# A hybrid decoder layer on one core: constant products in TensorE's pauses between the output projection and the first expert tile, and a refitted order

## The chip, the cores and the metric

The kernel runs on one core of one Trainium2 chip. The time is device time of one execution in microseconds, the median of several runs. The engines are TensorE (PE in the profile, its weight loads PEld), VectorE (DVE), ScalarE (ACT), GpSimd (POOL) and SyncE (SP, which here only issues DMAs). Each engine works through its own queue in order and waits for the others by semaphores.

## The reference

One layer over 512 tokens of width 1024, in float32. After a norm and one input projection, a state-space group (S5) and a sparse attention group work side by side. Their normed outputs meet in one output projection. A mixture of 32 experts follows, two per token.

```python
h = rms_norm(x, norm1_g[l])
proj = h @ w_in[l]
y_ssm = s5_mixer(proj[..., :D_SSM], ...)
y_att = nsa_mixer(proj[..., D_SSM:], ...)
mix = jnp.concatenate([rms_norm(y_ssm, out_g_ssm[l]), rms_norm(y_att, out_g_att[l])], axis=-1)
x = x + mix @ w_out[l]
x = x + hier_moe(rms_norm(x, norm2_g[l]), w_grp[l], b_grp[l], w_exp[l], b_exp[l],
                 w_gate[l], w_up[l], w_down[l])
```

In `hier_moe` a token's group is the one with the largest of 4 logits, and inside it the two best of 8 experts; each expert is `silu(t @ w_gate) * (t @ w_up)` times `w_down`.

## The kernel before

The tokens lie in four blocks of 128. Each part of the layer is a Python generator that yields one instruction (or a `Seq` of several) at a time: `proj`, `s5a`, `s5b`, `gelu`, `glu` (the gated unit behind S5), `scores`, `values`, `outproj`, `top2`, `route`, `expert` and others. `Sched.run` holds all live generators. At each step it works out for each one when its next instruction could start, by its own costs of instructions and the buffers' readiness, adds the generator's number from the table `PRIO`, and issues the one with the smallest sum. So the order on every engine is fixed when the program is built. In before.py `run` is at line 274, the table at 48.

`glu` multiplies by the gate's weights in PSUM tile `g` (`g<-yTh,gh` and so on), lets POOL add up the squares in `sq`, and multiplies them by a column of ones (`g<-ones,sq`). Behind it `wo` loads the weights of the output projection; `outproj` (line 1421) computes it in two parts, S5's first, attention's second, block by block into tiles `g` and `a`. `resid` adds the results to x on DVE.

`top2`, four times, transposes the new x of a block (`t<-ident`), multiplies it with the routing weights (128x36), and finds group and experts on DVE in many small steps. `norm2` makes the normed block on ACT, POOL and DVE and stores it to DRAM (`h2d`). `route` sums up positions with products of `A` and the constants `onesb` and `tri`, and from these the token list `gi` of 16 tiles: tile j serves experts j and j + 16, 64 tokens each. Its helper `weights` makes the table `tabw` with another eight products. `expert` (line 1705) gathers the tokens of a tile (`sc<-h2d,gi`), transposes them in two halves (`turn`), multiplies them with gate and up weights (16 products of 64 rows and 512 columns), then silu, transposes, and the down product. More tokens for an expert go to an overflow tile; `spill` computes its indices on DVE and, with `g<-R,oh`, on PE.

The expert weights are 96 tiles of 1 MB. `prefetch` issues their loads on SP in the order of use as soon as a buffer is free (pools `sa`, `sb`, `sc`, 26 of 1 MB, which the earlier parts share). An expert gives back two of them after each half of its gate products.

Of the kernel before, what the change touches and what calls it, by code (L numbers as in the profile page):

```python
# [27 lines left out]
for _n, _w in (("g1", 8), ("lre", 48), ("lim", 48), ("lst", 48), ("dsk", 8), ("bglu", 4), ("gq", 1),  # L28
# [9 lines left out]
NW = 10  # L38
NPS = 3, 2, 1, 2
NP = 4  # L40
DS = 1
SPILL_AT = 4
SC = 2, 4, 6, 8, 10, 12
# [1 line left out]

PRIO = {"proj": -3.72, "wsplit": 0.29, "xsplit": -0.08, "norm1": 0.04, "sink_u": 0.55, "sink_q": -0.76,
        "sink_gt": 3.61, "sink_k": -0.06, "s5": 0.19, "s5a": -0.69, "bcload": -9.42, "toeplitz": -18.02,
        "s5in": -0.17, "gelu": -0.12, "s5b": -0.75, "glu": -1.41, "compress": -0.96, "scores": -0.93,  # L50
        "scale": 0.37, "values": -0.25, "cmp": 0, "finish": -0.24, "wo": -1.28, "outproj": 0.02, "resid": -0.73,
        "norm2": -29.18, "top2": -0.61, "weights": 1.96, "place": -109.89, "prep": 1.2, "route": -1.71,
        "consts": -11.11, "scatter": -0.86, "base": -5.49, "moe": 43.94, "master": -5.48, "start": -35.5,
        "wload": -4.37, "prefetch": 3.58, "static": 2.45, "spill": -2.7}

# [54 lines left out]
class Sched:  # L112
# [12 lines left out]
    def spawn(self, gen, bias=0.0):  # L125
        self.th.append([gen, PRIO.get(gen.__name__, 0.0) + bias, None, None])

# [146 lines left out]
    def run(self):  # L274
        while self.th:
            moved = True
            while moved:
                moved = False
                for h in list(self.th):
                    while h[2] is None or callable(h[2]):  # L280
                        if h[2] is not None and not h[2]():
                            break
                        moved = True
                        try:
                            h[2] = next(h[0])
                        except StopIteration:
                            self.th.remove(h)
                            break
                        if isinstance(h[2], Seq):
                            h[3] = Seq()  # L290
                            h[3].extend(self.info(x[0]) for x in h[2])
                        else:
                            h[3] = None if callable(h[2]) else [self.info(x) for x in h[2]]
            best = None
            for h in self.th:
                if callable(h[2]):
                    continue
                _, s, f = self.pick(h)
                if best is None or s + h[1] < best[0]:
                    best = (s + h[1], s, f, h)  # L300
            if best is None:
                if self.th:
                    raise RuntimeError("stuck: " + ", ".join(
                        f"{h[0].__name__}:{h[0].gi_frame.f_lineno}" for h in self.th) )
                return
            self.cur = best[3][0]
            self.issue(best[1], best[2])
            best[3][2] = None
# [15 lines left out]
class Layer:  # L324
# [905 lines left out]
    def scores(self):  # L1230
# [38 lines left out]

        D = DS  # L1270
        for n in range(len(items) + D):
# [149 lines left out]
    def outproj(self):  # L1421
        V, S, G, T, Q = self.eng
        yield self.until("ys")
        for part in range(2):
            if part:
                yield self.until("ya")
            yh, yl, rs = (self.yah, self.yal, self.rsb) if part else (self.ysh, self.ysl, self.rsa)
            order = [(b, nh) for b in (3, 2, 1, 0) for nh in range(2)] if part else \
                [(b, nh) for nh in range(2) for b in (3, 2, 1, 0)]
            for b, nh in order:  # L1430
                if part:
                    yield self.until(f"ya{b}")
                i = 2 * part + nh
                yield lambda: i in self.wos
                hi, lo = self.wos[i]
                p = yield from self.ps(("g", "a") if part else "g", [128, 512])
                bs = slice(128 * b, 128 * b + 128)
                for k in range(0, 4, 2):
                    yield Seq(*(self.mm3(p, yh[:, i, bs], yl[:, i, bs], hi[:, i], lo[:, i], i == 0, i == 3)
                                for i in (k, k + 1)))  # L1440
                self.spawn(self.resid(p, rs, b, nh, part))
                if b == 0:
                    self.done(hi, lo)
                    if not part:
                        self.need["wo"] += 2
            self.done(yh, yl)
            if not part:
                self.flags.add("part0")

    def resid(self, p, rs, b, nh, part):  # L1450
        V, S, G, T, Q = self.eng
        if part:
            yield self.until(f"x{b}{nh}", f"r{b}")
        xv = self.xb[b][:, 512 * nh:512 * nh + 512]
        yield V.scalar_tensor_tensor(xv, p, rs[:, b:b + 1], xv, op0=OP.mult, op1=OP.add)
        self.done(p)
        self.flags.add(f"{'y' if part else 'x'}{b}{nh}")
# [247 lines left out]
    def expert(self, gi, oi, wv, ws, flag=None, tok=None):  # L1705

        V, S, G, T, Q = self.eng
        gx = yield from self.gather(gi)
        self.flags.add(flag)
        gT = yield from self.alloc("gT", [128, 8, 128])  # L1710
        yield from self.turn(gx, gT, 0)
        yield from self.turn(gx, gT, 1)
        self.done(gx)
        ph = yield from self.ps("a", [128, 512])
        for i in range(2):
            w = yield from ws(i)
            n = 128 // len(w)
            sls = [slice(n * s, n * s + n) for s in range(len(w))]
            yield Seq(*(T.matmul(ph[sl], gT[:, 4 * i + k, sl], wt[:, 512 * k:512 * k + 512],
                                 start=i + k == 0, stop=i == 1 and k == 3)  # L1720
                        for k in range(4) for sl, wt in zip(sls, w)))
            self.done(*w)
        self.done(gT)
        a = yield from self.alloc("h", [128, 256])
        yield S.activation(a, ph[:, 0:256], AF.Silu)
        yield V.tensor_mul(a, ph[:, 256:512], a)
        self.done(ph)
        aT = yield from self.alloc("hT", [128, 2, 128])
        pa = yield from self.ps("g", [128, 2, 128])
        yield Seq(*(T.transpose(pa[:, f], a[:, 128 * f:128 * f + 128], self.ident) for f in range(2)))  # L1730
        yield self.cp(aT, pa)
        self.done(pa, a)
        if tok is None:
            y = yield from self.alloc("z", [128, 1024])
        else:
            yh = yield from self.alloc("y", [128, 1024])
            yl = yield from self.alloc("y", [128, 1024])
        w = yield from ws(2)
        yield self.until("tabw")
        for nh in range(2):  # L1740
            py = yield from self.ps("a", [128, 512])
            yield Seq(*(T.matmul(py[sl], aT[:, f, sl], wt[:, 1024 * f + 512 * nh:1024 * f + 512 * nh + 512],
                                 start=f == 0, stop=f == 1) for f in range(2) for sl, wt in zip(sls, w)))
            c = slice(512 * nh, 512 * nh + 512)
            if tok is None:
                yield self.cp(y[:, c], py, wv)
            else:
                h = yh[:, c].bitcast(FR)
                yield S.activation(h, py, AF.Copy, scale=wv)
                yield V.scalar_tensor_tensor(yl[:, c].bitcast(FR), py, wv, h, op0=OP.mult, op1=OP.subtract)  # L1750
            self.done(py)
        self.done(aT, *w)
        if tok is None:
            yield self.until("base")
            yield G.indirect_dma_start(out=self.out, out_offset=bass.IndirectOffsetOnAxis(ap=oi, axis=0),
                                       in_=y, in_offset=None, compute_op=OP.add)
            self.done(y)
        else:
            self.spawn(self.scatter(tok, yh, yl))
# [222 lines left out]
def layer(ctx: ExitStack, tc: tile.TileContext, x, xt, win, pk, bcd, wglu, wck1, wck2, wcv1, wcv2,  # L1982
# [24 lines left out]
    L.hnq = [L.tmp.tile([128, 48], F32, name=f"hnq{i}") for i in range(2)]  # L2007
    L.need = {"P": NP, "ya": 2, "xs": 2, "comp": 2, "yT": 1, "ysl": 2, "wo": 5, "moe": 5, "spill": 0}
    L.keep = lambda: sum(L.need.values())
# [99 lines left out]
```

## Time and profile before

| what | us |
|---|---|
| median of 3 runs | 645.49 |
| lowest, highest | 645.2, 647.72 |
| the profiled execution | 649.24 |
| its span, first to last instruction | 647.4 |
| busy PE, DVE, ACT, POOL | 542.4, 369.0, 229.9, 126.5 |
| mean granted clock of TensorE | 0.916 |

Busy times are from the profile's first part; the profiled execution takes 1.8 us more than its span. A busy PE is not a PE at its peak: the same product takes twice the time at half the granted clock.

### The profile page before, as it was taken

The numbers are of one execution on the slowest core, as the hardware profiler recorded it, in microseconds if no ns is written. First come the engines' busy times: TensorE is split into PE (matmuls) and PEld (weight loads), VectorE is DVE, ScalarE is ACT, GpSimd is POOL, SyncE is SP. The second block draws the span as 40 slices with busy tenths as digits, with TensorE's granted clock in tenths as the row PEclk, the third lists the DMA queues.
The fourth block names the chain that finished last, engine by engine and source line by source line (L and its number), as shares of the span: only waits on it lengthen the run. The fifth ranks groups of instructions, "written<-read, shape, count | busy, mean of one in ns | idle before, by whom it ended". The sixth has DMA issues, their size and how long they took to land. (4 is left out here: it accounts for less than half of the span.)

```text
span 647.4 us, 8863 instructions
## 1 busy us (share of the span) xinstructions
PE 542.4 (84%) x3071; PEld 328.1 (51%) x3071; DVE 369.0 (57%) x1076; ACT 229.9 (36%) x513; POOL 126.5 (20%) x143
## 2 busy tenths in 40 slices
PE   3979968973968996999997369799999999999673
PEld 2869937862545665676686233344343443434120
DVE  6898989889897987978656951002141340414000
ACT  6425123453735764767233021124212122221001
POOL 1020110442620305003232021202101010211010
PEclk9979979995977997999999569989999999999887
DMA  6543444420201101614987958999999999999993
GB/s 202 156 134 102 112 123 114 135 62 8 42 5 36 42 26 58 266 66 139 411 344 265 376 195 313 382 391 386 420 388 397 409 387 420 387 420 352 326 316 53
DMA packets 39742, 148.40 MB, mean 229 GB/s; under 512 B 9488, under 2 KB 16528, under 8 KB 27024
## 3 DMA queue, kind: packets, MB, share of 16 engines
q1 hardware_dynamic: 32928, 129.46, 52.8%
q0 software_dynamic: 5040, 15.21, 9.5%
q10 hardware_dynamic: 1728, 3.15, 1.3%
q8 instruction: 25, 0.41, 0.3%
q14 instruction: 21, 0.17, 0.1%
HBM read 138.92 MB, written 13.60 MB: 236 GB/s over the span
## 5 line engine op out<-in xcount | busy, mean ns | idle before, releaser
L234 PE MATMUL a<-sa 128*128 128x256 f32 (+4 forms) x608 | 113.7, 330 | 18.9 <-ACT sa L234 14.5
L234 PEld LDWEIGHTS a<-sa 128*128 128x128 f32 (+1 forms) x608 | 86.8, 196 | 34.7 <-ACT sa L234 17.9
L234 PE MATMUL a<-sa,sb 128*64 128x512 f32 (+1 forms) x324 | 96.2, 594 | 1.3 <-DMA sa<-in_we 1.3
L234 DVE TENSOR_TENSOR h<-a,h 128x256 f32<-128x256 f32 x17 | 7.2, 425 | 132.2 <-ACT h L234 132.2
L234 PE MATMUL a<-sb 128*64 128x512 f32 (+1 forms) x204 | 73.5, 624 | 3.0 <-DMA sb<-in_we 3.0
L234 PE MATMUL a<-sa,hT 128*64 128x512 f32 (+1 forms) x168 | 57.0, 599 | 1.7 <-ACT hT L234 0.9
L234 PEld LDWEIGHTS a<-sa,sb 128*64 128x64 f32 (+1 forms) x324 | 29.5, 141 | 48.1 <-issue 45.4
L234 ACT ACTIVATE h<-a 128x256 f32<-128x256 f32 x17 | 6.5, 384 | 111.0 <-PE a L234 111.0
L234 POOL DMA_INDIRECT out<-sc,oi x10 | 16.0, 1600 | 124.9 <-ACT sc L234 80.2
L234 PEld LDWEIGHTS a<-sb 128*64 128x64 f32 (+1 forms) x204 | 22.0, 150 | 30.1 <-issue 24.8
L234 ACT ACTIVATE sb<-t 128x512 f32<-128x512 f32 x42 | 23.6, 595 | 23.2 <-PE t L234 22.8
L234 POOL DMA_INDIRECT sc<-h2d,gi x16 | 16.5, 1033 | 78.0 <-PE t L234 59.3
L234 PE MATMUL a<-sb,hT 128*64 128x512 f32 x80 | 30.1, 600 | 0.5 <-ACT hT L234 0.5
L234 ACT ACTIVATE sa<-a,mx 128x512 f32<-128x512 f32 (+3 forms) x48 | 27.1, 573 | 8.5 <-DVE mx L234 7.9
L234 PE MATMUL o<-sa 128*128 128x256 f32 x192 | 28.4, 284 | 1.1 <-DVE xr L234 1.1
L234 DVE SCALAR_TENSOR_TENSOR sa<-a,tabw,sa 128x512 fp32r<-128x512 f32 x12 | 9.0, 751 | 35.5 <-ACT sa L234 25.5
L234 DVE TENSOR_REDUCE mx<-a 128x1 f32<-128x512 f32 (+3 forms) x44 | 27.0, 635 | 3.0 <-PE a L234 3.0
L234 PE MATMUL g<-sb,sa 128*128 128x512 f32 x104 | 27.7, 404 | 0.0
L234 ACT ACTIVATE pts<-t 128x512 f32<-128x512 f32 (+1 forms) x35 | 20.4, 595 | 18.1 <-PE t L234 18.1
L234 PE MATMUL t<-ident,sc 128*128 128x128 f32 x136 | 21.7, 306 | 5.3 <-DMA sc<-h2d,g1i 4.1
L234 PEld LDWEIGHTS o<-sa 128*128 128x128 f32 x192 | 25.3, 191 | 1.6 <-DVE xr L234 1.5
L234 PEld LDWEIGHTS t<-ident,sc 128*128 128x128 f32 x136 | 16.6, 155 | 18.4 <-issue 13.0
(391 smaller groups left out, 1046.3 us busy)
## 6 DMA issues: line engine op xcount, KB each, us to landing
sa<-in_we SPq DMA_DIRECT2D x58, 1024.0 KB, 22.6
sb<-in_we SPq DMA_DIRECT2D x33, 1024.0 KB, 16.4
raw<-in_win SPq DMA_DIRECT2D x14, 512.0 KB, 3.8
sc<-in_we SPq DMA_DIRECT2D x5, 1024.0 KB
sb<-in_wout SPq DMA_DIRECT2D x6, 512.0 KB, 7.4
xr<-in_xt SPq DMA_DIRECT2D x4, 512.0 KB, 5.3
sa<-in_wck SPq DMA_DIRECT2D x8, 256.0 KB, 3.0
sa<-in_wcv SPq DMA_DIRECT2D x8, 256.0 KB, 3.6
```

Of the source, the lines that this page charges most:

```text
L234: inst = getattr(e.real, fn)(*a, **k)
```

## The change

A generator `warm` is added. It is started when the last products of the output projection's second part are issued (block 0, second half). It takes one of the three PSUM tiles `a` and yields, again and again, eight products of the constants `onesb` and `tri` (128x128, bfloat16), until a flag is set that the first half of an expert's tokens is transposed. Nothing reads what they compute. `run` treats it apart: it is issued only if its earliest start plus 0.3 comes before the earliest start of every other generator on any engine. Besides, 14 of the numbers in `PRIO` are new, and the order changes with them; the table's rows tell little, two stand here.

```diff
+WARM = 8
...
-PRIO = {"proj": -3.72, "wsplit": 0.29, "xsplit": -0.08, "norm1": 0.04, "sink_u": 0.55, "sink_q": -0.76,
+PRIO = {"warm": 0.3, "proj": -19.73, "wsplit": 0.29, "xsplit": -0.08, "norm1": 0.04, "sink_u": 0.55, "sink_q": -0.76,
...
-            best = None
+            best = idle = None
+            first = 1e9
             for h in self.th:
                 if callable(h[2]):
                     continue
                 _, s, f = self.pick(h)
+                if h[0].__name__ == "warm":
+                    idle = (s + h[1], s, f, h)
+                    continue
+                first = min(first, s)
                 if best is None or s + h[1] < best[0]:
                     best = (s + h[1], s, f, h)
+            if idle and idle[0] < first:
+                best = idle
...
                 if b == 0:
                     self.done(hi, lo)
                     if not part:
                         self.need["wo"] += 2
+                    elif nh:
+                        self.spawn(self.warm())
...
+    def warm(self):
+
+        T = self.eng[3]
+        p = yield from self.ps("a", [128, 512])
+        while "turned" not in self.flags:
+            yield Seq(*(T.matmul(p[:, 0:128], self.onesb, self.tri, start=True, stop=True) for _ in range(WARM)))
+        self.done(p)
...
         yield from self.turn(gx, gT, 0)
+        self.flags.add("turned")
         yield from self.turn(gx, gT, 1)
```

PE, behind the end of the gated unit, before (`oss`: squares of the attention's output; `pts`: transposed attention weights):

```order
L234 MATMUL g<-yTl,gh 128x512
L234 MATMUL g<-yTh,gl__2453 128x512
L234 MATMUL g<-ones,sq 128x1 x4
L234 MATMUL t<-ident,sa 128x128 x16
L234 MATMUL o<-pts,sa 64x512 x2
L234 MATMUL t<-ident,sa 128x128 x8
L234 MATMUL t<-ones,oss 128x1
L234 MATMUL a<-sa 128x256 x4
```

The products with `ones` follow the unit's last product directly.

The same place on PE in the change:

```order
L235 MATMUL g<-yTl,gh 128x512
L235 MATMUL g<-yTh,gl__2636 128x512
L235 MATMUL o<-pts,sa 64x512 x2
L235 MATMUL t<-ident,sa 128x128 x8
L235 MATMUL o<-pts,sa 64x512 x2
L235 MATMUL t<-ident,sa 128x128 x8
L235 MATMUL a<-sa 128x256 x4
L235 LDWEIGHTS identb
L235 MATMUL a<-cneg,identb 128x2x128
...
L235 MATMUL o<-pts,sa 64x512 x2
L235 MATMUL g<-ones,sq 128x1 x4
```

Three pairs of value products, two groups of eight transposes and two score blocks (the second is left out here) now stand ahead of the products with `ones`.

PE at the first expert, before (`sc` under `t<-ident` is the gathered tokens, `R,oh` the overflow tile's indices):

```order
L234 MATMUL g<-sa 128x48
L234 MATMUL t<-ident,sc 128x128 x16
L234 MATMUL a<-sa,sb 64x512 x8
L234 MATMUL g<-R_4023,oh 128x2 x4
L234 MATMUL a<-sb 64x512
```

The same place on PE in the change:

```order
L235 MATMUL g<-sb 128x48
L235 MATMUL t<-ident,sc 128x128 x4
L235 LDWEIGHTS onesb
L235 MATMUL a<-tri,onesb 128x128
...
L235 MATMUL t<-ident,sc 128x128 x8
L235 MATMUL a<-sa,sb 64x512 x8
L235 MATMUL a<-sb 64x512
...
L235 MATMUL t<-ident,sc 128x128 x8
L235 MATMUL a<-sa,sb 64x512 x8
L235 MATMUL g<-R_4292,oh 128x2 x4
```

Between the first four transposes and the next eight stands the last block of eight added products. Both halves of the first expert's products now come before the second expert's remaining transposes, and the overflow's indices behind the second expert's first eight products.

On DVE the gating product of the first expert (`h<-a,h`) stands behind the table's sum in the change, ahead of the overflow's indices, which came first before:

```order
L235 TENSOR_REDUCE tabw<-g 128x16
L235 TENSOR_TENSOR h<-a,h 128x256
L235 TENSOR_SCALAR tt<-ov_137,it 128x32
L235 TENSOR_SCALAR se<-tt 128x32
L235 TENSOR_TENSOR t_4262<-tt,ovn 128x32
```

On SP three stores of the residual (`out<-sb`) stand behind 13 weight loads in the change, where two stood behind ten and the third behind twelve.

## Rows read from the trace of the kernel before

**Rows 1.** The page's slices, 40 equal parts of the span, in tenths.
```profile
PE   3979968973968996999997369799999999999673
...
PEclk9979979995977997999999569989999999999887
```

**Rows 2.** Stretches: length, busy PE, PEld, DVE, ACT, POOL (instructions), granted clock, DMA share, GB/s.
```profile
240.00:256.00 16.00, 10.57 (x48) 8.50 (x48) 11.08 (x22) 6.21 (x12) 8.53 (x7) 0.86 0.01 2
...
352.00:368.00 16.00, 4.98 (x28) 4.38 (x29) 12.23 (x83) 2.70 (x8) 2.50 (x2) 0.56 0.98 369
368.00:384.00 16.00, 6.51 (x49) 4.54 (x50) 12.67 (x69) 3.13 (x8) 3.66 (x4) 0.50 0.62 214
384.00:400.00 16.00, 16.00 (x80) 5.79 (x78) 1.08 (x6) 2.42 (x4) 3.46 (x4) 0.98 0.76 271
...
576.00:592.00 16.00, 16.00 (x78) 7.06 (x74) 6.98 (x11) 3.10 (x5) 5.42 (x5) 1.00 1.02 387
```

**Rows 3.** The chain that ended last: start, us, what.
```profile
581.41 32.91 DMA sa<-in_we
```

**Rows 4.** Time line of PE: start, us, what [idle before, what ended it].
```profile
352.24 0.66 PE L234 MATMUL t<-ident,sb 128*128 128x128 f32 x4 [0.84 <-DVE sb L234]
...
360.03 0.18 PE L234 MATMUL g<-A,onesb 128*128 128x32 bf16 x1 [0.78 <-DVE sb L234]
...
365.97 0.18 PE L234 MATMUL g<-A,tri 128*128 128x32 bf16 x1 [4.92 <-DVE A L234]
...
369.67 0.47 PE L234 MATMUL g<-sa 128*128 128x16 bf16 x12
...
377.25 0.71 PE L234 MATMUL g<-sa 128*128 128x48 bf16 x8 [5.86 <-DVE sa L234]
377.78 1.09 PE L234 MATMUL t<-ident,sc 128*128 128x128 f32 x4
380.11 2.95 PE L234 MATMUL t<-ident,sc 128*128 128x128 f32 x12 [1.23 <-DMA sc<-h2d,gi]
382.99 4.46 PE L234 MATMUL a<-sa,sb 128*64 128x512 f32 x16
...
396.48 3.65 PE L234 MATMUL a<-sa,sb 128*64 128x512 f32 x16
```

**Rows 5.** Time line of SP: the first weight load that an expert released.
```profile
387.49 0.33 SPq L234 DMA_DIRECT2D sa<-in_we  x1
```

**Rows 6.** Waits of PE up to 352 us: total us, times, longest.
```profile
PE g L234 <- POOL sq L234: 5.4, 1, 5.4
```

**Rows 7.** Time line of PE around the end of the gated unit.
```profile
247.16 0.39 PE L234 MATMUL g<-yTh,gl__2453 128*128 128x512 f32 x1
252.98 1.86 PE L234 MATMUL g<-ones,sq 128*128 128x1 f32 x8 [5.43 <-POOL sq L234]
254.70 3.75 PE L234 MATMUL t<-ident,sa 128*128 128x128 f32 x16
258.39 1.08 PE L234 MATMUL o<-pts,sa 128*64 128x512 f32 x4
259.40 1.09 PE L234 MATMUL t<-ident,sa 128*128 128x128 f32 x8
...
261.71 1.65 PE L234 MATMUL g<-sb,sa 128*128 128x512 f32 x6
...
267.82 4.45 PE L234 MATMUL g<-sb,sa 128*128 128x512 f32 x18
```

**Rows 8.** Stretches of 2 us at the clock's fall and rise.
```profile
354.00:356.00 2.00, 0.38 (x2) 0.38 (x2) 0.00 (x0) 1.64 (x5) 0.84 (x1) 0.50 0.87 223
...
384.00:386.00 2.00, 2.00 (x12) 0.57 (x10) 0.00 (x0) 1.05 (x1) 0.60 (x1) 0.84 0.92 352
```

**Rows 9.** Time line of DVE: the overflow's indices, first and last large step.
```profile
378.12 0.23 DVE L234 TENSOR_SCALAR tt<-ov,it 128x32 f32<-128x32 f32 x1
...
382.55 0.69 DVE L234 TENSOR_TENSOR oh<-io,pe 128x512 f32<-128x512 f32 x1
```

More of the change, by code (lines that the diff above doesn't have):

```diff
@@ L44 @@
 CH = "kc", "u0", "u1", "k0", "k1", "gt", "q0", "q1"
-PRIO = {"proj": -3.72, "wsplit": 0.29, "xsplit": -0.08, "norm1": 0.04, "sink_u": 0.55, "sink_q": -0.76,
[L49 to L54, printed above, removed]
+PRIO = {"warm": 0.3, "proj": -19.73, "wsplit": 0.29, "xsplit": -0.08, "norm1": 0.04, "sink_u": 0.55, "sink_q": -0.76,
+        "sink_gt": 4.55, "sink_k": -0.06, "s5": 0.19, "s5a": -0.69, "bcload": -9.42, "toeplitz": -18.37,
+        "s5in": -0.41, "gelu": -0.13, "s5b": -0.75, "glu": -1.41, "compress": -0.96, "scores": -0.93,
+        "scale": -0.59, "values": -0.25, "cmp": -0.42, "finish": -0.24, "wo": -1.28, "outproj": 0.66,
+        "resid": -0.73, "norm2": -29.18, "top2": -0.61, "weights": 1.96, "place": -109.49, "prep": 1.2,
+        "route": -0.92, "consts": -11.18, "scatter": -4.3, "base": -5.49, "moe": 43.94, "master": -10.82,
+        "start": -35.5, "wload": -4.84, "prefetch": 3.58, "static": 2.45, "spill": -2.7}
 class Eng:
```

## The prediction

> **What bounds the kernel now.** I read the slices of the span first, then the table of 16 us stretches, then the waits and the time lines of the places where TensorE (PE) is not full, and last the chain that ended last.
>
> The slices show PE nearly full outside four places, and a granted clock that falls wherever PE has been idle [rows 1]. One such place is 240 to 256 us, with PE, VectorE (DVE) and the DMA engines all below their share; the longest is the routing, 352 to 384 us, where DVE is the busy engine and PE is asked for 4.98 and 6.51 of 16 us [rows 2]. Behind it the DMA share is 1.02 [rows 2], and the chain at the end holds 32.91 us of waiting for a weight load although PE had been working without a pause before it [rows 3]. So the end of the kernel is set by when the stream of 1 MB weight tiles gets going. That stream has stopped at the end of the routing because every buffer is full: at 387.49 SP issues a load again, just when the first expert's first 16 matmul records (382.99 and 4.46 us) have freed a buffer [rows 4, 5]. The reader should take two things from this. A microsecond by which the first expert comes earlier is a microsecond at the end. A microsecond of PE work inside the expert stage is worth nothing.
>
> Up to 352 us the time is PE's and DVE's: whatever idle time goes there moves the routing, the first expert and the end together.
>
> **The sum, against the profiled execution** (649.24 us, span 647.4). It stands 3.75 us above the median of the runs, 645.49, so I make the sum as a difference and take it from both. About 0.5%, 3.2 us, is what a measurement of this kernel can tell from no change.
>
> *A, the order before the routing.* The list of waits has one row in which PE stands still for POOL: 5.4 us [rows 6]. The time line says what it is: the last matmul of the gated unit starts at 247.16, the sum of squares that POOL adds up comes at 252.98, and the four products with `ones` (1.86 us) stand in PE's queue ahead of everything else [rows 7]. In the new order seven groups stand between them, as the first two fences of the section on the change show. Priced by the same time line (two value products 1.08, eight transposes 1.09 [rows 7]; the two score blocks I take at 0.9 each, an estimate between those two) they are three times 1.08, twice 1.09 and twice 0.9, 7.2 us. That is more than 5.4, so the wait is covered. The clock adds to it: after the wait 16 transposes take 3.75 us, where eight at full clock take 1.09 [rows 7], so 1.6 us, and half of 1.86 for the products with `ones`, 0.9 us. Value: 5.4, the wait alone. Ends: 7.9 with the clock's part, and 0 if another wait takes its place (second rival). The rest of the new order up to 352 us I cost at nothing: the first 80 or so groups on PE stand as before, and DVE loses some copies and gains some scalings. The ends for that are 3 us either way, an estimate from some ten instructions of 0.2 to 0.7 us (such as in [rows 9]) that change engines.
>
> *B, the clock in the routing.* From 354 to 384 us the granted clock is 0.50, the lower of the two levels, 1.2 GHz; at 384 to 386 it is on its way back to 2.4 [rows 8]. PE works only 11.5 of 32 us there [rows 2], and nearly all of that is waited for by nobody: DVE is busy 12.23 and 12.67 of each 16 us [rows 2] with one chain of small steps. What is on the path is the piece from 377.78 on: the transposes of the first gathered tokens and the first expert's products. In the old order 16 transposes of two experts come first; the last 12 start at 380.11, after a gather, and end in 382.99, where the products begin: 2.88 us [rows 4]. In the new order the first expert's products follow after 12 transposes in all, and at full clock eight take 1.09 [rows 7]. With about 0.6 for the copy in between, the products start between 380.5 (nothing waits for the second gather) and 381.2 (it does), 1.8 to 2.5 us earlier. The products themselves: 16 records take 3.65 us at full clock against 4.46, 0.8 us [rows 4]. Value 2.5; ends 0.8 (only the products gain) and 5.7 (half of all 11.5 us).
>
> *C, the added products.* 240 pairs of a weight load and a 128-column bf16 product, in blocks of 24, 24, 72, 8, 8, 96 and 8. They wait for nothing, so a block starts when PE gets there and runs through. The four long ones stand where PE now idles 0.84, 0.78, 4.92 and 5.86 us [rows 4]. What one pair costs the trace doesn't show. From below: 18 products of 512 columns take 4.45 us, 247 ns each, so 128 columns 62 ns [rows 7]. From above, at the lower clock, twice as much, 124 ns. Does the load come on top? At the lower clock 12 loads with products of 16 columns take 0.47 us together [rows 4], under 40 ns a pair, so a load hides or is short; I take 62 ns. The blocks are then 1.5, 1.5, 4.5 and 6.0 us long, and what hangs over the gaps is 0.7, 0.7, 0 and 0.1 us. The first overhang delays transposes whose copies ScalarE (ACT) takes late anyway; the others I count: 0.8 us.
>
> If the load did not hide, it would add at full clock no more than half of those 40 ns: 82 ns a pair, blocks of 2.0, 2.0, 5.9 and 7.9 us, and without the first overhang 4.2 us late instead of 0.8. That is the third rival.
>
> The Trainium skill, TensorE: Matmul & The Clock Gate, section Back-to-back issue gap, speaks for that side: it puts a sustained stream of load and product pairs at 128 columns at about 81 ns each, well above the gap of the products alone. By it C would be 4 us instead of 0.8. No row here has such pairs at full clock.
>
> *D, the overflow expert's indices.* DVE computes them from 378.12 to the table written at 382.55 (0.69 us), 5.1 us [rows 9]; the new order puts the first expert's gating product ahead of them on DVE. The small products that need the table stand on PE after eight transposes (1.09) and eight products of the second expert (3.65), 4.7 us after the first expert's products; the table is there no sooner than 5.1 us after them. PE stalls 0.4 us or more, and behind it stands the second expert. I take 0.5.
>
> Sum: -5.4 - 2.5 + 0.8 + 0.5 = -6.6. The profiled execution would take 642.6 us, and the median 645.5 - 6.6 = **638.9 us**.
>
> **Rivals.**
> 1. *More than the wait.* A at its end of 7.9 and the 3 us of the order for it: 645.5 - 13 = 633. For: the slow transposes stand right behind the wait. Chance 0.14.
> 2. *Another wait takes its place.* The output projection's weights are loaded only after the gated unit is done; its first products start at 261.71, 14.2 us after the last product of the unit [rows 7]. The new order has 7.2 us of work before the `ones` products, 0.9 for themselves, and behind them, ahead of the projection's first, eight more groups, 7.5 by the same prices: 15.6, so the margin is 1.4 us only. If the copies that this work needs come late, PE waits there instead: A is 0, the time 645.5 - 1.2 = 644.3, the same by the measure. Chance 0.21.
> 3. *The load shows.* The products run at full clock, but a pair takes 82 ns: the second block holds the routing's step for 1.2 us, the third for 1.0, and the fourth the tokens' transposes for 2.0. C is 4.2 and the sum -3.2: 642.3. For: nothing in the rows has such pairs at full clock. Against: the 12 pairs in 0.47 us [rows 4]. Chance 0.09, on the edge between faster and the same. The page named under C has this price for its pairs.
> 4. *The clock isn't held* (the change doesn't do what it says). The pairs then take 124 ns at worst: the four blocks 3.0, 3.0, 8.9 and 11.9 us in the gaps of 0.84, 0.78, 4.92 and 5.86, 14.4 us over; B is 0. Even with A the sum is -5.4 + 14.4 + 0.5 = +9.5: 655. The point from which it decides: with B gone, 216 pairs less 12.4 us exceed 4.9 us from 80 ns a pair on. Against: wherever PE's slice is full the clock's is too [rows 1], and the blocks fill the routing's pauses. Chance 0.08.
> 5. *The stream starts later.* The prefetch of weights before the routing goes ahead of three stores of the residual instead of between them; if loads then lie ahead of the stores of the normalised tokens, which the gathers wait for, each of 1 MB costs 2.7 us at 387 GB/s [rows 2]. Four of them are 10.8 us, the sum +4.2 and the time 649.7; the point from which the kernel is slower than before is two and a half. For: the order on SP. Against: loads that go ahead of the stores of the residual should also be through earlier. Chance 0.06.
>
> **How the numbers follow.** The forecast has 0.42. Faster by more than 3.2 us: 0.42, rival 1 and half of rival 3, 0.61 in round numbers. Same: rival 2 and the other half, 0.25. Slower: rivals 4 and 5, 0.14. The range for 8 in 10 reaches from 631 (A 7.9, B 3.3, 3 for the rest of the order, C and D nothing) to 648 (rival 2, and 3 lost by the rest of the order); it leaves out the slower rivals. The forecast's own is 635 to 642.
>
> **What would show it.** In the profile after: no wait of PE for POOL's sum of squares; the first output projection products some 5 us earlier on PE; a granted clock near 1.00 through the routing, with PE busy there; the tokens' transposes starting without a pause right behind the added products only if these hang over; the first expert's 16 records in 3.65 us, starting 7 to 9 us earlier; the DMA share at 1.02 from some 7 us earlier to the end. I am wrong if the routing begins no earlier, if its granted clock still shows 0.50, or if the end doesn't follow the first expert.

## The result, and the profile after

| | before | changed |
|---|---|---|
| median of four runs | 646.61 us | 638.93 us |
| lowest, highest | 645.2, 647.78 | 637.65, 641.49 |
| profiled execution, its span | 649.24, 647.4 | 640.01, 638.1 |
| mean granted clock | 0.916 | 0.943 |

The ratio is 0.9887, with an interval from 0.9844 to 0.9931: 7.3 us faster (4.5 to 10.1); the medians differ by 7.7. Timed again beside other kernels, the change gave 0.9909 (0.9879 to 0.9940). The eleven executions of the changed kernel in these two timings fall into two groups, five of 636.3 to 637.9 us at a mean granted clock of 0.947 to 0.954 and six of 639.6 to 642.5 us at 0.941 to 0.943; the execution profiled here is of the second group, and the one profiled for the repeat of the first.

The 16 us stretches of the changed kernel, to be read against [rows 2] (the columns are the same: length, then PE, PEld, DVE, ACT and POOL with their counts, granted clock, DMA share, GB/s):

```profile
240.00:256.00 16.00, 15.23 (x71) 10.51 (x70) 13.04 (x27) 11.02 (x24) 4.84 (x5) 1.00 0.17 60
352.00:368.00 16.00, 10.53 (x164) 10.11 (x164) 14.47 (x93) 0.60 (x4) 0.68 (x2) 0.89 0.90 343
368.00:384.00 16.00, 14.42 (x150) 9.16 (x147) 5.36 (x30) 4.26 (x8) 3.97 (x4) 1.00 0.71 260
384.00:400.00 16.00, 15.82 (x71) 5.84 (x72) 5.10 (x24) 2.74 (x5) 3.12 (x3) 0.89 0.93 351
400.00:416.00 16.00, 11.99 (x57) 4.98 (x54) 0.00 (x0) 2.53 (x5) 4.24 (x3) 0.88 1.02 372
```

The last of them before the change, which [rows 2] leave out:

```profile
400.00:416.00 16.00, 15.13 (x72) 4.86 (x68) 0.85 (x2) 3.68 (x6) 2.67 (x2) 1.00 1.02 379
```

At 240 to 256 us PE has 15.23 instead of 10.57 us of work. In the routing its work is doubled by the added pairs (a weight load and a product each), and the granted clock is 0.89 and 1.00 instead of 0.56 and 0.50 (0.79 and 1.00 in the profile of the repeat). The DMA share is 0.93 in 384 to 400 us, against 0.76 before [rows 2]; in 400 to 416 us it is 1.02 in both. So the stream of weights gains by running better up to 400 us, not by an earlier full share.

The longest waits of PE between 144 and 352 us (us in total, times, longest), to be read against [rows 6]:

```profile
PE g L235 <- DVE w L235: 7.5, 4, 4.4
PE a L235 <- ACT sa L235: 6.0, 10, 1.2
PE g L235 <- DVE sa L235: 3.6, 1, 3.6
```

The wait for POOL's `sq` is gone from the list; the waits for ACT's `sa` have grown from 3.3 to 6.0 us and those for DVE's `w` from 4.9 to 7.5.

PE's time line at the places that the prediction spoke of (start, length, in brackets the idle time before it), against [rows 4, 7]:

```profile
265.00 1.05 PE L235 MATMUL g<-ones,sq 128*128 128x1 f32 x8
...
273.18 2.03 PE L235 MATMUL g<-sb,sa 128*128 128x512 f32 x6
...
349.36 1.51 PE L235 MATMUL a<-tri,onesb 128*128 128x128 bf16 x24
...
352.98 1.51 PE L235 MATMUL a<-tri,onesb 128*128 128x128 bf16 x24
...
354.70 4.18 PE L235 MATMUL a<-tri,onesb 128*128 128x128 bf16 x72
...
360.57 0.18 PE L235 MATMUL g<-A,tri 128*128 128x32 bf16 x1 [1.65 <-DVE A L235]
...
364.48 0.18 PE L235 MATMUL g<-A,tri 128*128 128x32 bf16 x1 [3.66 <-DVE A L235]
364.50 1.02 PE L235 MATMUL a<-tri,onesb 128*128 128x128 bf16 x8
...
366.92 5.88 PE L235 MATMUL a<-tri,onesb 128*128 128x128 bf16 x96
372.63 0.36 PE L235 MATMUL g<-sb 128*128 128x48 bf16 x8
...
374.75 3.65 PE L235 MATMUL a<-sa,sb 128*64 128x512 f32 x16
...
384.18 0.63 PE L235 MATMUL t<-ident,sc 128*128 128x128 f32 x4 [1.76 <-DMA sc<-h2d,gi]
384.74 5.34 PE L235 MATMUL a<-sa,sb 128*64 128x512 f32 x16
390.01 1.05 PE L235 MATMUL g<-R,oh 128*128 128x2 f32 x8
```

The reader should see five things. The products with `ones` stand at 265.00, with no idle time before them. The first products of the output projection come at 273.18, not 5 us before the old 261.71 but 11.5 behind it. The pairs follow each other every 56 ns (24 of them from 349.36 to the next instruction at 350.71), every 59 ns where a block begins at the lower clock (96 from 366.92 to 372.63), and the 8 at 364.50, behind 3.66 us of idle time, every 101 ns. The first expert's products start 8.2 us before the old 382.99. And the indices of the overflow tile (`R,oh`) come at 390.01, 2.6 us behind the old 387.37. DVE begins to compute these only at 382.67, behind the first expert's gating product, where it began at 378.12 before [rows 9]:

```profile
373.03 0.21 DVE L235 TENSOR_REDUCE tabw<-g 128x16 f32<-128x48 f32 x1 [0.74 <-PE g L235]
...
382.67 0.24 DVE L235 TENSOR_SCALAR tt<-ov,it 128x32 f32<-128x32 f32 x1
```

The granted clock around the pairs at 349.36, at 364.50 and at the start of the block of 96 (366.92):

```profile
350.00:352.00 2.00, 2.00 (x28) 2.00 (x25) 1.93 (x14) 1.31 (x3) 0.86 (x1) 1.00 0.86 344
...
364.00:365.00 1.00, 0.52 (x7) 0.52 (x7) 0.66 (x5) 0.04 (x1) 0.00 (x0) 0.64 1.01 422
365.00:366.00 1.00, 1.00 (x22) 0.91 (x21) 0.79 (x3) 0.15 (x1) 0.00 (x0) 0.50 1.06 442
...
367.00:368.00 1.00, 1.00 (x17) 1.00 (x14) 0.88 (x5) 0.00 (x0) 0.27 (x1) 0.65 0.00 0
```

What lies behind 384 us differs between executions of this one program. In the profile of the repeat the second expert's products take 3.65 us instead of 5.34, and the indices come 3.5 us sooner, 1.9 us more than the first expert (373.15):

```profile
382.91 3.65 PE L235 MATMUL a<-sa,sb 128*64 128x512 f32 x16
386.50 1.05 PE L235 MATMUL g<-R,oh 128*128 128x2 f32 x8
```

### The profile page after: what moved, and what is told of

It reads as the page before. It is cut to its first block, busy times and chain, and to the rows that moved or that the text cites. A ratio compares the mean times of both kernels' runs of the same rounds, so it can differ in the third digit from the quotient of the medians.

```text
span 638.1 us, 9321 instructions
## 1 busy us (share of the span) xinstructions
PE 552.2 (87%) x3311; PEld 336.3 (53%) x3311; DVE 370.3 (58%) x1080; ACT 227.9 (36%) x509; POOL 124.6 (20%) x143
## 5 line engine op out<-in xcount | busy, mean ns | idle before, releaser
L235 PE MATMUL a<-sa 128*128 128x256 f32 (+4 forms) x608 | 116.6, 331 | 20.9 <-ACT sa L235 17.5
L235 PE MATMUL a<-sa,sb 128*64 128x512 f32 (+1 forms) x296 | 108.2, 615 | 3.8 <-DMA sa<-in_we 3.8
L235 PE MATMUL a<-sb 128*64 128x512 f32 x200 | 82.6, 615 | 2.5 <-DMA sb<-in_we 2.5
L235 PE MATMUL a<-sa,hT 128*64 128x512 f32 (+1 forms) x152 | 49.8, 600 | 0.5 <-ACT hT L235 0.5
L235 PEld LDWEIGHTS a<-sb 128*64 128x64 f32 x200 | 23.7, 140 | 32.7 <-issue 29.2
L235 POOL DMA_INDIRECT out<-sa,oi x10 | 16.0, 1599 | 123.6 <-ACT sa L235 98.8
L235 ACT ACTIVATE sa<-a,tabw 128x512 f32<-128x512 f32 (+1 forms) x32 | 22.0, 688 | 42.8 <-PE a L235 41.7
L235 PE MATMUL a<-sb,hT 128*64 128x512 f32 x72 | 34.0, 599 | 0.5 <-ACT hT L235 0.5
L235 PE MATMUL t<-ident,sa 128*128 128x128 f32 (+1 forms) x160 | 25.9, 290 | 3.5 <-ACT pts L235 2.1
L235 PEld LDWEIGHTS t<-ident,sa 128*128 128x128 f32 (+1 forms) x160 | 17.8, 141 | 16.3 <-ACT pts L235 7.6
```

What stands on the lines that cost most here:

```text
L235: inst = getattr(e.real, fn)(*a, **k)
```

## The experiments

Theory to begin with: the order pays through the sum of squares and through ScalarE's waits for stores in the routing, the pairs pay through the clock at the first expert. The rivals: the order alone, or the pairs alone. Each run is given by its ratio to the kernel before, timed beside it, with the interval. This table has the places in the profiles on which the readings rest (us): the end of the last product of the output projection, the start of the gating table's products, the start of the first expert's, and the span.

| kernel | output projection ends | table | first expert | span | ratio |
|---|---|---|---|---|---|
| before | 351.4 | 377.3 | 383.0 | 647.4 | |
| before, again | 351.5 | 376.0 | 380.6 | 644.8 | |
| changed | 349.5 | 372.6 | 374.8 | 638.1 | 0.9887 |
| changed, again | 347.8 | 371.0 | 373.2 | 635.0 | 0.9909 |
| order without pairs | 350.4 | 372.9 | 376.6 | 641.8 | 0.9950 |
| refit alone | 349.0 | 371.5 | 376.1 | 637.1 | 0.9893 |
| pairs alone | 352.4 | 379.6 | 381.8 | 645.5 | 0.9992 |
| square elsewhere | 352.2 | 376.5 | 381.4 | 644.7 | 1.0008 |
| early priorities | 345.6 | 369.1 | 374.4 | 637.5 | 0.9823 |
| output projection late | 371.0 | 388.8 | 400.9 | 661.2 | 1.0258 |
| pairs in the refit's order | 348.1 | 372.2 | 374.8 | 635.8 | 0.9881 |
| early with pairs | 344.1 | 368.8 | 370.9 | 632.9 | 0.9870 |
| wait put back | 352.5 | 375.9 | 380.9 | 640.9 | 0.9965 |
| pairs doubled | 349.0 | 383.6 | 386.2 | 650.1 | 1.0080 |

From the first expert's products to the end all fourteen profiles need 260.0 to 265.2 us, while that start moves over 30 us. Where medians of different timings are compared, the reader should keep in mind that the median of the kernel before moved between them, from 645.6 to 647.1 us.

**Order without pairs.** The scheduler counts the pairs, but they aren't issued:

```diff
-        inst = getattr(e.real, fn)(*a, **k)
+        inst = None if self.cur.__name__ == "warm" else getattr(e.real, fn)(*a, **k)
```

> The changed kernel with its order of every other instruction kept, and the 240 added pairs left out. Theory (the pairs pay through the clock at the first expert): the granted clock is 0.50 from some 355 us to the first expert; the products that write the gating table start where they do now or up to 0.5 us earlier (nothing hangs over them), the first expert's 16 products start 1 to 2 us later and take 4.5 instead of 3.65 us, and the time is some 2 us above the changed kernel's, 5 to 6 below the kernel before. Rival 1 (the order alone brings it): the time is the changed kernel's, 7 to 8 below before. Rival 2 (the pairs bring most): 2 or less below before.

Measured: 642.57 us, 0.9950 (0.9931 to 0.9970). PE's time line in it:

```profile
372.88 0.71 PE L235 MATMUL g<-sb 128*128 128x48 bf16 x8 [5.82 <-DVE sb L235]
...
376.57 4.72 PE L235 MATMUL a<-sa,sb 128*64 128x512 f32 x16
...
390.88 1.05 PE L235 MATMUL g<-R,oh 128*128 128x2 f32 x8 [1.55 <-DVE R L235]
```

From the table to the first expert it is 3.69 us instead of 2.12, and the products take 4.72 instead of 3.65. Taking the pairs out of this order costs 3.0 to 3.6 us by the medians (against either timing of the changed kernel) and 2.6 to 4.1 by the ratios, a little more than expected.

**Refit alone.** The line that starts `warm` is taken out, the new priorities stay.

> The new priorities without the added pairs, and the scheduler not knowing of them: up to the products for the gating table the order is the changed kernel's, and the first expert comes behind 16 transposes and the second gather as in the kernel before. Theory: routing as in the run above, then 5.7 us from the gating table's products to the first expert's as in the kernel before; the time is 3.3 us above the changed kernel's, some 4.5 below before. Rival 1 (the place of the first expert's products is worth nothing): same as the run above. Rival 2 (the pairs bring most): 2 or less below before.

Measured: 638.74 us, 0.9893 (0.9872 to 0.9914): the changed kernel's time. The theory falls here. PE's time line:

```profile
371.51 0.70 PE L235 MATMUL g<-sb 128*128 128x48 bf16 x8 [5.86 <-DVE sb L235]
...
376.07 4.28 PE L235 MATMUL a<-sa,sb 128*64 128x512 f32 x16
380.27 1.05 PE L235 MATMUL g<-R,oh 128*128 128x2 f32 x8
```

The first expert starts 1.3 us later than in the changed kernel and takes 4.28 us, at a lower clock in part; but the overflow's indices are there at 380.27, 9.7 us earlier (6.2 against the repeat), since DVE computes them straight behind the table. In the order without pairs the first expert starts only 0.5 us later and the indices come at 390.88; it is 3.8 us slower. The two orders differ only around the first two experts, so this difference is what that place costs. How it does is seen on PE and on SP. Without pairs PE waits 1.55 us for the indices, the second expert's remaining products behind them run at a granted clock of 0.57, and SP, which waits for these products, issues its next weight load 4.45 us later than in the refit alone. Order without pairs, then refit alone:

```profile
392.00:396.00 4.00, 4.00 (x12) 1.18 (x12) 0.63 (x5) 0.38 (x1) 0.00 (x0) 0.57 0.94 313
```

```profile
397.51 0.33 SPq L235 DMA_DIRECT2D sc<-in_we  x1
```

```profile
393.06 0.33 SPq L235 DMA_DIRECT2D sc<-in_we  x1
```

This load stands at 394.95 in the changed kernel, at 391.44 in its repeat, and in two kernels further down at 391.18 (pairs in the refit's order) and 406.05 (pairs doubled). From it to the end these six profiles need 243.2 to 244.6 us, where the first expert's start leaves 261.0 to 265.2. So with the new numbers the end follows the second expert's products more closely than the first's. The other order at the first expert, which the scheduler chooses when it counts the pairs and with them on a fast PE, costs about as much as the pairs give back.

**Pairs alone.** The changed code with the old table of priorities (and `warm` at 0.3).

> The old priorities with the added pairs: up to the products for the gating table the order is that of the kernel before, the first expert's products come ahead of the second's transposes as in the changed kernel. Theory: routing as late as before (the table's products near 377.5 us), the first expert's products some 2.1 us behind them instead of 5.7, and the time some 3.3 us below before. Rival 1 (the order alone brings it): time as before. Rival 2 (the pairs also speed up the routing): 5 or more below before.

Measured: 645.38 us, 0.9992 (0.9971 to 1.0014): nothing, where 3.3 us were expected.

```profile
361.23 4.48 PE L235 MATMUL a<-tri,onesb 128*128 128x128 bf16 x72
...
373.17 6.64 PE L235 MATMUL a<-tri,onesb 128*128 128x128 bf16 x96
379.64 0.36 PE L235 MATMUL g<-sa 128*128 128x48 bf16 x8
```

The last block hangs over: the table's products start 1.72 us behind the start of the DVE instructions that feed them (377.92), where they start 0.41 behind it without pairs. The gain at the first expert (2.12 us from the table instead of 4.6 to 5.7) is, as far as the profile shows, used up by this and by the overflow's indices, which come at 395.00 instead of 387.37.

**Square elsewhere.** The kernel before in its own order:

```diff
+        if self.cur.__name__ == "norm2" and AF.Square in a:
+            a = self.junk, *a[1:]
         inst = getattr(e.real, fn)(*a, **k)
...
-        self.ss = n([128, 4, 4], F32)
+        self.ss, self.sched.junk = n([128, 4, 4], F32), n([128, 512], BF)
```

> The kernel before in its own order; only the squares that ScalarE sums up for the second norm go to a scratch tile of 128 x 512 bf16 and no longer into the tile whose store to DRAM must have landed first. Theory (DVE's wait of 3.23 us for ScalarE at 356.21 us is on the path, and its end in the changed kernel is a part of the gain of its own): that wait is gone, the gating table's products start 3 us earlier, and the time is some 3 us below before. Rival (the stores of the normalised tokens, behind the same tile, hold the gather instead): the table's products come earlier but the first gather does not, and the time is as before.

Measured: 645.98 us, 1.0008 (0.9993 to 1.0023). This expectation failed, by another way than the rival's. DVE's wait is gone, but PE now waits 3.46 us for DVE ahead of the routing's products, against 0.78 in [rows 4]:

```profile
359.10 0.19 PE L236 MATMUL g<-A,onesb 128*128 128x32 bf16 x1 [3.46 <-DVE sb L236]
```

The next wait, 4.91 us, is as before. From the end of the output projection to the first gather's issue it is 20.4 us, against 22.4 and 20.7 in the two profiles of before. So DVE's wait lay for the most part beside another chain; which one was not followed up.

**Before again.** No edit.

> The kernel before, unchanged, profiled a second time, to see how far two profiles of one program lie apart. Theory (the profile of before that the prediction was summed against was a slow one, 3.7 us above the median): span 642 to 645, bytes still to move at 400 us about 89 MB instead of 89.9, and the first expert's products within 1 us of 383.0. Rival: the same as the first profile, and the runs of the pairs alone and of the square elsewhere lie truly below it at 400 us.

Measured: a span of 644.8 us, and in its trace:

```profile
376.02 0.71 PE L234 MATMUL g<-sa 128*128 128x48 bf16 x8 [5.87 <-DVE sa L234]
...
380.62 3.65 PE L234 MATMUL a<-sa,sb 128*64 128x512 f32 x16
```

The first expert starts 2.4 us earlier than in [rows 4], and its products take 3.65 instead of 4.46 us, the length that they have at full clock, with no pairs. The row on which the prediction put 0.8 us was that of one execution. The profile that the sum was made against was a long one, as the theory said; the first expert moved by more than the 1 us that it allowed.

**Early priorities.** Before, with the new priorities for everything but `outproj`, `route`, `place` and `scatter`. **Output projection late.** The reverse: these four new, all others old. Of the four only the output projection's number counts: with it alone changed, the order on every engine is the same, both here and between the refit alone and the early priorities.

> The kernel before with the new priorities for all but the output projection, the routing, the placing and the scattering; no pairs. The products with the sum of squares then stand behind the work of the changed kernel, the output projection has its old priority. Theory (the covered wait for the sum of squares pays): no wait of PE for POOL's sum of squares, PE's idle time up to 256 us 5.7 us below before, the time 3 to 5 us below before. Rival (what pays is the output projection's later place): 1 us or less below before, because the idle time comes back between 256 and 352 us.

> The kernel before with the new priority of the output projection (0.66 instead of 0.02; also of the routing, the placing and the scattering) and nothing else; no pairs. PE still waits 5.4 us for POOL's sum of squares. Theory (the covered wait pays): 1 to 2 us below before at most. Rival (what pays is the output projection's later place): 4 us or more below before, with the stores of the normalised tokens landing before ScalarE's next squares need their tile.

Measured: 636.84 us, 0.9823 (0.9795 to 0.9852), and 663.39 us, 1.0258 (1.0223 to 1.0292). The part with the covered wait pays 11 us alone, more than the whole change and more than the 3 to 5 expected; the other, of which at most 1 to 2 us of gain were expected, alone costs 17. PE with the early priorities:

```profile
264.87 1.05 PE L234 MATMUL g<-ones,sq 128*128 128x1 f32 x8
...
273.06 2.00 PE L234 MATMUL g<-sb,sa 128*128 128x512 f32 x6
...
345.17 0.39 PE L234 MATMUL a<-sb,sa 128*128 128x512 f32 x1
```

Summed over the 16 us stretches up to 256 us, PE is idle 6.7 us less than before, and up to 336 us still 6.1 less; the output projection ends 5.8 us earlier. In the refit alone it is 5.8 us less up to 256 us, but only 3.4 up to 336, and the projection ends 2.4 earlier. In the run with only the output projection's priority changed, SP shows why loads suffer:

```profile
315.83 12.28 SPq L234 DMA_DIRECT2D sa<-in_we  x6
339.05 33.11 SPq L234 DMA_DIRECT2D out<-sb  x4
```

Its four stores of the residual are issued over 33 us from 339.05 on, and the weight loads stand behind them in SP's queue: the DMA share is 0.00 in 360 to 368 us. SP waits there for the residual on DVE, and this for the projection, which itself ends 19.6 us later than before: on PE its last 24 product records stand behind one product of the routing, which waits 6.12 us for DVE. The two lines of PE, and the stretch without loads:

```profile
362.39 0.19 PE L234 MATMUL g<-A,tri 128*128 128x32 bf16 x1 [6.12 <-DVE A L234]
...
370.61 0.40 PE L234 MATMUL a<-sb 128*128 128x512 f32 x1
```

```profile
360.00:368.00 8.00, 5.61 (x17) 4.54 (x17) 6.14 (x32) 0.20 (x1) 1.81 (x1) 0.56 0.00 1
```

**Pairs in the refit's order.** The pairs are issued where PE is free, but don't enter the scheduler's count of PE's time:

```diff
+    wf = 0.0
...
+        if self.cur.__name__ == "warm":
+            self.wf = max(self.wf, s) + 0.06
+            return getattr(e.real, fn)(*a, **k)
...
                 if h[0].__name__ == "warm":
+                    s = max(s, self.wf)
```

> The new priorities with pairs in the gaps, but the scheduler not counting them, so that the first expert's order is that of the run without pairs (both tokens' transposes, then its products, the overflow indices ahead on VectorE). Theory (what the pairs give through the clock is eaten by the other order of the first expert, with the later overflow indices): the first expert's products start 1 us earlier than in the run without pairs and take 3.65 us, and the time is 1 to 2 us below the changed kernel's. Rival (the pairs hang over by as much as they give): the changed kernel's time.

Measured: 640.29 us, 0.9881 (0.9854 to 0.9909); the refit alone has 0.9893. The first expert starts 1.3 us earlier and takes 3.65 us, as expected, and SP's load behind the second expert comes 1.9 us earlier. But the time is neither below the refit alone nor the 1 to 2 us below the change that were expected, by what can be measured: this expectation failed, and what the pairs are worth outside the changed order stays open between nothing and some 3 us. The order differs from the refit's in some places behind the third expert.

**Early with pairs, and the change again.** The changed kernel with the four old priorities; and the changed kernel as it is.

> The changed kernel with the old priorities of the output projection, the routing, the placing and the scattering (0.02, -1.71, -109.89, -0.86): the run of the early priorities with 248 pairs in blocks of 16, 32, 40, 24, 8, 8, 112 and 8, and the first expert's products ahead of the second's transposes. Theory (the pairs and the order that comes with them cancel, as in the new order): the time of the run of the early priorities, 9 to 11 us below before. Rival 1 (the pairs bring the recorded 2.5 us): 12 us or more below before. Rival 2 (the overflow indices behind the first expert cost more than the clock gives): 8 or less below before.

> The changed kernel, unchanged, timed beside the others and profiled a second time. Theory: 0.9887 of the kernel before as at first, within 0.004, so that the two runs with the old priority of the output projection lie 3 us or more below it. Rival (the difference is one between chips): equal to these.

Measured: 637.61 us, 0.9870 (0.9851 to 0.9890), and 639.61 us, 0.9909 (0.9879 to 0.9940). Without the pairs it was 0.9823: they add nothing there either, and may cost. The run with the early priorities and pairs lies 2.0 us below the change timed beside it, by the medians, where 3 or more were expected. The kernel with the early priorities alone is the fastest, 0.9823 against the change's 0.9887 and 0.9909.

**Wait put back.** The early priorities in the same order; POOL repeats its last product for the sum of squares:

```diff
+    muls = 0
...
+        if self.cur.__name__ == "glu" and e.key == "G" and fn == "tensor_mul":
+            self.muls += 1
+            for _ in range(6 if self.muls == 4 else 0):
+                getattr(e.real, fn)(*a, **k)
```

> The run of the early priorities in the same order on all engines, but POOL makes the last product for the sum of squares seven times instead of once, 6 times 1.1 us more, so that PE gets to the products with the sum of squares some 5 us before it is there. Theory (the covered wait is what the early priorities pay by): PE waits 5 us there again, the output projection ends some 5 us later than in the run of the early priorities (345.2 us in its trace), and the time is 4 to 7 us above it. Rival (other parts of the order pay): less than 2 us above it.

Measured: 642.93 us, 0.9965 (0.9947 to 0.9983), 6.1 us above the early priorities by the medians, 9 by the ratios (4 to 7 were expected). Its waits and its time line on PE:

```profile
PE g L240 <- POOL sq L240: 5.4, 1, 5.4
```

```profile
270.26 1.86 PE L240 MATMUL g<-ones,sq 128*128 128x1 f32 x8 [5.38 <-POOL sq L240]
271.99 1.20 PE L240 MATMUL a<-sa 128*128 128x256 f32 x4
...
352.11 0.39 PE L240 MATMUL a<-sb,sa 128*128 128x512 f32 x1
```

```profile
270.00:272.00 2.00, 1.74 (x9) 1.74 (x9) 0.22 (x1) 0.00 (x0) 0.21 (x1) 0.50 0.00 0
```

With the same 5.4 us of idle time as before the change, the `ones` products and those behind them run at half the clock again (granted clock 0.50; 1.86 us instead of 1.05), and the projection ends 6.9 us later. The covered wait is most of what the early priorities pay by.

**Pairs doubled.** The changed kernel, each pair issued twice.

> The changed kernel in its own order, each of the 240 pairs made twice: 480, at 58 ns the blocks take 3.0, 3.0, 8.4 and 11.8 us instead of 1.5, 1.5, 4.2 and 5.9. Theory (the blocks fill the gaps to the brim, what hangs over is paid in full): the second block hangs over by 1.5, the third by 2 to 2.5, the last by 5.5 to 6 us; the products for the gating table start 8 to 10 us later than in the changed kernel (372.6 us), and the time is 7 to 10 us above it. Rival (there is slack behind the pairs): less than 4 us above it.

Measured: 651.41 us, 1.0080 (1.0051 to 1.0108), 11.8 us above the changed kernel timed beside it, where 7 to 10 were expected. The added 240 pairs are 13.4 us at 56 ns; the table's products start at 383.63, 11.0 and 12.6 us later than in the two profiles of the change. Little of it is hidden: the single pairs had filled the gaps.

## Why the prediction was right, and where it was not

The forecast of 638.9 us is the median measured, and that it is met so closely is luck. It was a gain of 6.6 us taken from 645.5, the median of three runs, where four runs have 646.61; the gain measured is 7.3 us (4.5 to 10.1). Inside it errors of several us cancelled. The order without the pairs is worth 6.9 us (refit alone, 0.9893), where A has 5.4; the pairs, with the order at the first expert that comes with them, are worth about nothing, where B, C and D together have 1.2.

By places, in the first pair of profiles (in brackets the second): the output projection ends 1.9 us earlier (3.7), the way from there to the table is 2.8 us shorter (1.3), the way from the table to the first expert 3.6 (2.5), and the rest 1.1 (2.4). So the wait's 5.4 us are not all there at the end of the output projection, and the routing before the table, on which the prediction put nothing, gained too.

*A, the order before the routing (-5.4).* The mechanism is shown: the wait is gone, and putting it back in the same order costs 6 to 9 us, above the 5.4 taken and around the end of 7.9 with the clock's part. The early priorities pay 11 us in all. The step that failed is the next one: the rest of the new order "I cost at nothing", because the first 80 groups stand as before. The output projection's priority went from 0.02 to 0.66, and refit alone (0.9893) and early priorities (0.9823) differ in order by that number alone: 4.5 us lost by the ratios. It isn't what moves the projection's first products 11.5 us back, since they start at 273.06 with the old number as well. It lets PE's idle time come back behind them, between 256 and 336 us, and the projection end 3.4 us later. The ends of 3 us given for the rest of the order were a little too narrow.

*B, the clock in the routing (-2.5).* With the order held, the pairs are worth some 3 us (2.6 to 4.1), and the first expert's start moves by 1.6 to 1.8 us beside 1.1 in its products: the step was right in kind and size. But it came with an order that loses as much, so the term as a part of this change is about nothing: refit alone and the change have the same time. The row for the products' 4.46 us was also one execution's; the second profile of before has 3.65.

*C, the added products (+0.8).* Right. A pair takes 56 ns at full clock and 59 to 61 ns over the block of 96, whose first pairs still run at the lower clock (62 taken). The last block hangs over by 0.5 to 0.7 us in the two profiles of the change (0.1 taken; measured from the start of the DVE instructions that feed the table's products, less the 0.41 us without pairs). Behind the second block PE waits 0.16 us for DVE all the same, and the products behind the third are followed by 1.65 us of waiting for DVE.

*D, the overflow's indices (+0.5).* Mis-sized. It was priced as a stall of PE at one instruction. In fact DVE starts the whole chain 9.6 us behind the table's sum (373.03, 382.67), PE stalls elsewhere as well (1.76 us for the second gather at 384.18), and in this execution the clock falls again (0.89 in 384 to 400 us; in the repeat it is 1.00 there). In the run without pairs this order costs 3.8 us: the wait for the indices is 1.55 us, and with the lower clock behind it SP's next load comes 4.45 us later.

*The end follows the first expert.* Shown only within 5 us over all profiles. Order without pairs and refit alone start it 0.5 us apart and end 4.7 us apart in their profiles; in the six profiles with all the new numbers the end follows the weight load behind the second expert's products within 1.5 us. "A microsecond of PE work inside the expert stage is worth nothing" thus fails for the second expert's products.

Rival 1 (more than the wait) comes near for the early priorities alone (11 us against the 10.9 it has for A and the order), not for the change. Rival 2 (another wait takes its place) was half true: 2.3 us of the idle time came back by 336 us, as waits for ACT and DVE (`sa`, `pts`, `sb`) and not for the output projection's weights. Rival 3 (the load shows) is out by the pairs' own rows. Rival 4 (the clock isn't held) is out but for the 0.89 of 352 to 368 us (0.79 in the repeat), where the scheduler left 1.65 and 3.66 us without pairs. Rival 5 (the stream starts later) did not happen: the first gather is issued at 367.73 instead of 373.83. Of the signs given, two were wrong: the output projection's first products are not 5 us earlier (rival 2's own count of 15.6 us of work ahead of them already put them later than before), and the DMA share is not full 7 us earlier, only higher on the way there.

## What to carry to other kernels

Price each moved group of a refitted order by itself, and the ones that land later above all: here a gain of 11 us and a loss of 4 to 5 stood in one table of numbers, and neither was visible in the sum. Work that only keeps the clock up is worth what its order leaves: it must fit its gap (13.4 us of it too much cost 11.8), and a scheduler that counts on the faster clock may choose an order that gives the gain back. Take a second profile of the kernel before and of the change, since a row of one execution can be off by as much as the term that rests on it (0.8 us here before, 1.7 after).

## What the runs showed of the hardware

Pairs of a weight load and a 128-column bf16 product, back to back with the same weights, start 56 ns apart at the granted clock 1.00 (24 from 349.36 to 350.71), and 101 ns apart at 364.50, behind 3.66 us of idle time, where the granted clock is 0.64 and 0.50. That is below the 62 ns which the prediction estimated for such a product without its load, so next to nothing of the load can come on top. The Trainium skill, TensorE: Matmul & The Clock Gate, section Back-to-back issue gap, gives about 81 ns for a sustained stream of such pairs, and about 56 for a product alone; these runs agree with the second figure for pairs, where the weights are always the same tile.

Two profiles of one program lay 2.6 and 3.1 us apart in span (before, and the change), with the first expert's start 2.4 and 1.6 us apart; 1.2 and 1.7 us of this were there by 265 us already.
